# Attention's causal mask: added in place to the kept row F instead of by matmuls, with masks, minima and exponentials issued at high priority

## The chip, the core and the metric

The kernel runs on one core of one Trainium2 chip. The core has a matrix engine, TensorE (PE, with its weight loads shown apart as PEld), a vector engine, VectorE (DVE), a scalar engine, ScalarE (ACT), a general engine, GpSimd (POOL), a synchronisation engine, SyncE (SP), from whose queue most transfers are issued, and 16 DMA engines. Work lies in SBUF (128 partitions) and in PSUM, where PE writes its products. The metric is the device time of one execution in microseconds (us). A profile is one further execution, recorded by the hardware profiler.

## What is computed

One layer with two branches over a sequence of 1024 positions and a width of 1024: a Mamba-2 state-space branch and an attention branch with a forget gate, merged by sigmoid gates, projected and normalised. The change is in the attention branch only, which has 16 heads of 64:

```python
def _forgetting_attention(q, k, v, log_f):
    ...
    fcum = jnp.cumsum(log_f, axis=-1)
    ...
        s = jnp.einsum('bhqd,bhkd->bhqk', q[:, :, q0:q1], k[:, :, :q1]).astype(jnp.float32) * scale
        s = s + fcum[:, :, q0:q1, None] - fcum[:, :, None, :q1]
        qpos = q0 + jnp.arange(ATT_BLOCK)
        kpos = jnp.arange(q1)
        s = jnp.where(kpos[None, :] <= qpos[:, None], s, -jnp.inf)
        prob = jax.nn.softmax(s, axis=-1)
        outs.append(jnp.einsum('bhqk,bhkd->bhqd', prob.astype(v.dtype), v[:, :, :q1]))
```

F is `fcum`, the running sum of the log forget gate. The term F[t] of the query is the same for a whole row of the softmax and drops out of it; what is left is the row -F[s] over the keys, and the mask: a key later than the query counts for nothing. With blocks of 128 queries only the block on the diagonal needs the mask, and there it is always the same triangle.

## The kernel before, and the names that the change touches

**Order of the work.** Tile, the framework, schedules instructions per engine by priority and by estimated times; priority is the order in the program unless `tc.high_priority()` raises it. Some instructions are kept in program order on their engine: `mm` (matmuls, all recorded at line 130), `turn` (transposes on PE, line 133) and whatever stands in `pin(...)`. So PE's order is written out by hand, while ACT, DVE and POOL are arranged by the scheduler around it.

**The weight stream.** All projections go through `Stream`, a list of steps with seven products each (a Strassen scheme in 2 x 2 blocks). `half()` issues half a step: six matmuls of 128 x 512. Their weights are made just before: the weight or a sum of weights (`raw`, `sum`; lines 357, 373 and 381) is split into a high part `wop` (line 351, ACT) and a low part (line 352, DVE). The inputs are split alike (`x6h` and its kin; lines 280 and 281). Results in PSUM (`pb`, `pc`, `pd`) are taken out by `keep` (line 404, ACT, tile `s` in SBUF) and `give` (lines 412 on ACT, 414 to 418 on DVE).

**The attention loop.** Attention and the stream share PE. The loop runs over 48 groups: 8 head pairs `hp` (heads 2 hp and 2 hp + 1, in the two halves of the partitions, e = 0, 1) with six groups g each. A group has two query blocks i (u = 0, 1) and one half h of the keys (512 of them):

```python
GROUPS = [((7, 6), 1), ((7, 6), 0), ((5, 4), 1), ((5, 4), 0), ((3, 2), 0), ((1, 0), 0)]
```

The groups g = 0, 2, 4 and 5 of every pair hold the diagonal: 32 groups, 64 blocks i, 128 tiles of scores. Their widths are 512 (u = 0) and 384 (u = 1) for g = 0 and 4, and 256 and 128 for g = 2 and 5; the other groups have two widths of 512. For each group, in this order:

- `scores` (line 1438) for u = 0, then for u = 1. For both heads: three matmuls (high by high, high by low, low by high) into a PSUM tile `s` (four buffers, shared with the transposes' `pt`). On the diagonal two more in bfloat16 per head: `far` by `eye`, which add 1e30 (scores are kept with their sign turned) to the keys beyond the query, the last 128 columns of the width. Then line 1466 on DVE: it adds the row of F, `fb`, writes the sum to `ex` and its minimum over the row to `nm`. Then line 1470 on ACT: the exponential of `nm - ex`, in place, with its sum to `sm`.
- `fill(m, 0)`: two or three halves of the stream on PE, while DVE and ACT do the minima and the exponentials.
- `turned` (line 1472): transposes of `ex` on PE into `pt`, copied to `p` by ACT (line 1501) or DVE (line 1499). A transpose for u needs that block's exponential.
- `fill(m, 1)`: further halves, and in the next turn of the loop `weighted`, the product of `p` with the values.

**F.** `load_k` loads keys and, last, `fb[hp, h]`: the two heads' rows of F, 512 wide, the same for all partitions (128 x 2 x 512, 512 KB), by line 1335 on SP's queue. There is one buffer for each h. `load_k(hp + 1, 1)` is called at g = 2 and `load_k(hp + 1, 0)` at g = 5, in `loads`, which is called before `turned`. `load_q` (line 1326) loads queries; tiles x4l and the like are inputs of the stream, loaded at line 265.

**Setting up the mask.** Before the loop `eye` (an identity moved by 64 rows, so that each head's half of the partitions can contract it) and `far` (a triangle of 1e30) are made by two memsets, two `affine_select` on POOL and four copies.

Of the kernel before, what the change touches and what calls it, by code (L numbers as in the profile page):

```python
# [8 lines left out]
F32 = mybir.dt.float32  # L9
F32R = mybir.dt.float32r  # L10
BF16 = mybir.dt.bfloat16
AF = mybir.ActivationFunctionType
ALU = mybir.AluOpType
# [3 lines left out]
P = 128  # L17
# [9 lines left out]
NEG = -1.0e30  # L27
# [59 lines left out]
def hybrid_layer(ctx: ExitStack, tc, a, out):  # L87

    nc = tc.nc
# [5 lines left out]
    ident = const.tile([P, P], F32, name="ident")  # L95
# [33 lines left out]
    def mm(*args, **kw):  # L129
        return tc.keep_in_program_order(nc.tensor.matmul(*args, **kw))  # L130
# [4 lines left out]
    def pin(op):  # L135
        return tc.keep_in_program_order(op)

    def small(name="th"):
        return gp.tile([P, HALF], F32, tag="th", name=name)
# [316 lines left out]
    class Stream:  # L456
# [73 lines left out]
        def half(self):  # L530
            if self.run is None:
                if self.at == len(self.steps):
                    return False
                p, which = self.steps[self.at]
                if which == 7 and p.ops is ops_a and "merged" not in fin:
                    return False
                if p.ops is ops_a and not all(p.ops.ready(OPERAND[which].strip("-"), j) for j in range(KH)):
                    return False
                self.ahead(False)
                for ops in self.building:  # L540
                    ops.some(OPERAND[which])
                self.run = p.do(which)
                next(self.run)
            else:
                for _ in self.run:
                    pass
                self.run = None
                p, which = self.steps[self.at]
                if p in self.following:
                    ops = self.following[p]  # L550
                    if ops not in self.building:
                        self.building.append(ops)
                    ops.open(OPERAND[which])
# [581 lines left out]
    with tc.tile_pool(name="pro", bufs=1, reuse_waits="tile", side="right") as pro, tc.tile_pool(  # L1135
        name="prop", bufs=1, space=PSUM, reuse_waits="tile", side="right"
# [114 lines left out]
    with tc.tile_pool(name="ssm", bufs=1, reuse_waits="tile", side="right") as sp, tc.tile_pool(  # L1251
        name="ssmp", bufs=1, space=PSUM, reuse_waits="tile", side="right"
# [42 lines left out]
    with tc.tile_pool(name="att", bufs=1, reuse_waits="tile", side="right") as ap, tc.tile_pool(  # L1295
        name="attp", bufs=1, space=PSUM, reuse_waits="tile", side="right"
    ) as pp:
        rows = [slice(64 * e, 64 * e + 64) for e in range(2)]

        eye = ap.tile([P, 192], BF16, name="eye")  # L1300
        far = ap.tile([P, 192], BF16, name="far")
        nc.vector.memset(eye, 0.0)
        big, beyond = small("big"), small("beyond")
        nc.vector.memset(big[:, 0:192], -NEG)
        for e in range(2):
            nc.vector.tensor_copy(eye[rows[e], 64:P], ident[rows[e], rows[e]])
            nc.gpsimd.affine_select(
                beyond[:, 192 * e : 192 * e + 192], big[:, 0:192], [[1, 192]], ALU.is_gt, 0.0, base=64 * e - 64,
                channel_multiplier=-1,
            )  # L1310
            nc.vector.tensor_copy(far[rows[e], :], beyond[rows[e], 192 * e : 192 * e + 192])

        corner = [(eye[:, 64:192], far[:, 64:192]), (eye[:, 0:P], far[:, 0:P])]

# [5 lines left out]
        q, k, v, fb = {}, {}, {}, {}  # L1320

        def load_q(hp, pair):

            t = ap.tile([P, 2, 256], F32R, tag="q", bufs=2, name="q")
            for n, dram in enumerate((qh_dram, ql_dram)):
                nc.sync.dma_start(t[:, n, :].bitcast(F32), dram[hp, :, pair[1] * P : pair[1] * P + 256])
            q[hp, pair] = t

        def load_k(hp, h):

            t = k[hp, h] = ap.tile([P, 2, HALF], F32R, tag=f"k{h}", name="k")
            for n, dram in enumerate((kh_dram, kl_dram)):
                nc.sync.dma_start(t[:, n, :].bitcast(F32), dram[hp, :, half(h)])
            f = fb[hp, h] = ap.tile([P, 2, HALF], F32, tag=f"fb{h}", name="fb")
            nc.sync.dma_start(f, f_dram[2 * hp : 2 * hp + 2, half(h)].unsqueeze(0).to_broadcast([P, 2, HALF]))

        def load_v(hp, h):
            v[hp, h] = ap.tile([P, 4, P], F32, tag=f"v{h}", name="v")
            pin(nc.sync.dma_start(v[hp, h], v_dram[hp][:, 4 * h : 4 * h + 4, :]))
# [98 lines left out]
        def scores(hp, g, u):  # L1438

            pair, h = GROUPS[g]  # L1440
            i = pair[u]
            w = min(HALF, (i + 1) * P - h * HALF)
            s = [pp.tile([P, HALF], F32, tag="s", bufs=4, name="s") for e in range(2)]
            t, keys = q[hp, pair], k[hp, h]
            isl = slice(i % 2 * P, i % 2 * P + P)
            ops = [(t[:, x, isl], keys[:, y, 0:w]) for x, y in ((0, 0), (0, 1), (1, 0))]
            diagonal = h == i // 4
            for m, (x, y) in enumerate(ops):
                for e in range(2):
                    mm(  # L1450
                        s[e][:, 0:w], x[rows[e]], y[rows[e]], start=(m == 0), stop=(m == 2 and not diagonal),
                        skip_group_check=True,
                    )
            if diagonal:
                for n, (x, y) in enumerate(corner):
                    for e in range(2):
                        mm(
                            s[e][:, w - P : w], x[rows[e]], y[rows[e]], start=False, stop=(n == 1),
                            skip_group_check=True,
                        )  # L1460
            hd = heads[hp]
            for e in range(2):
                o = ex[:, e, u, 0:w]
                nm = hd.at(hd.nm, i, h, e)
                pin(
                    nc.vector.tensor_tensor_reduce(  # L1466
                        o, s[e][:, 0:w], fb[hp, h][:, e, 0:w], 1.0, 3.0e38, ALU.add, ALU.min, nm
                    )
                )
                pin(nc.scalar.activation(o, o, AF.Exp, scale=-1.0, bias=nm, accum_out=hd.at(hd.sm, i, h, e)))  # L1470

        def turned(hp, g, sent):

# [46 lines left out]
        def fetched(name, j):  # L1520
            y = small("y")
            nc.sync.dma_start(y, ops_a.block(name, j))
            return y

        def difference_tile():
            return ap.tile([P, HALF], F32, tag="x", bufs=1, name="x")
# [44 lines left out]
        def loads(m):  # L1571

            hp, g = divmod(m, 6)
            more = hp + 1 < NK
            if g == 0:
                if hp:
                    load_v(hp, 0)
                if not m:

                    for j in range(KH):  # L1580
                        stream.line += ops_s.differences(j, difference_tile, small)
            if g == 1:
                load_q(hp, (3, 2))
            if g == 2 and more:
                load_k(hp + 1, 1)
            if g == 3:
                load_q(hp, (1, 0))
                if more:
                    load_v(hp + 1, 1)
                if hp >= KH:  # L1590
                    state["t"] = difference_tile()
                    nc.sync.dma_start(state["t"], ops_a.block("t1", hp - KH))
            if g == 4 and more:
                load_q(hp + 1, (7, 6))
            if g == (5 if more else 4) and hp >= KH:
                state["y"] = fetched("b11", hp - KH)
            if g == 5 and more:
                load_k(hp + 1, 0)
                load_q(hp + 1, (5, 4))
# [12 lines left out]
            load_v(0, h)  # L1612
        for _ in range(14):
            stream.half()

        weights = (1.1, 1.1, 1.1, 1.1, 0.75, 0.95, 1.05, 0.85)

# [10 lines left out]
        for m in range(6 * NK + 1):  # L1628
# [9 lines left out]
            hp, g = divmod(m, 6)  # L1638
            if not g:
                heads[hp] = Heads(hp)  # L1640
            for u in range(2):
                scores(hp, g, u)
# [86 lines left out]
```

## Time and profile before

| | before |
|---|---|
| median of 3 runs | 1298.21 us |
| lowest and highest run | 1296.74, 1300.02 us |
| the profiled execution, device time | 1301.24 us |
| its span in the trace | 1299.5 us |
| mean granted clock of TensorE in it | 0.995 |
| stage with the attention loop | about 686 to 1140 us |
| mask matmuls (first 687.0, last 1136.7 us) | 256, 18.4 us busy |
| minima, line 1466 | 192, 95.7 us busy on DVE |
| exponentials, line 1470 | 192, 116.0 us busy on ACT |

In the rows below, a group of instructions is given by line, engine, operation, out<-in by the program's names and the shape; "x256" is the number of instructions. Rows of a timeline begin with the start in us from the span's start and the duration (of x instructions run together, overlaps not counted twice); a bracket at their end gives the idle time just before on that engine and the instruction that ended it. "216/221/229" are shortest, median and longest duration in ns. Rows of the chain of waits give start, length and what the end of the kernel was waiting for in that time.

### The profile page before, as it was taken

Reading aid. Unit: us, or ns where it says so; the run is one execution under the profiler, and the core shown is the slowest. Engines: PE = TensorE matmul, PEld = TensorE weight load, DVE = VectorE, ACT = ScalarE, POOL = GpSimd, SP = SyncE. Lnnn points to the kernel's source line nnn. Section 1 sums busy time; section 2 is a strip of 40 time slices with the busy share of each in tenths; the row PEclk is TensorE's granted clock in tenths of the full one; section 3 lists DMA queues with packets and bytes.
Section 4 is the critical chain, followed back from the end, with each engine's and each line's share of the span. In section 5 each row is a group of like instructions: output and inputs, shape, how many; then the busy total and the mean of one; then the engine's idle time right before and its main releaser. Section 6 shows DMA issues by size and latency. Waiting matters only on the chain.

```text
span 1299.5 us, 20991 instructions
## 1 busy us (share of the span) xinstructions
PE 1257.2 (97%) x7054; PEld 984.8 (76%) x7054; DVE 1002.6 (77%) x1994; ACT 789.0 (61%) x1738; POOL 260.1 (20%) x250
## 2 busy tenths in 40 slices
PE   5999999999999999999999999999999999899997
PEld 3678878887888888878877777777667777678786
DVE  7989886897788888897676666766687677786875
ACT  7745665565665666576546566566675566653654
POOL 3000430014300331024001121110001102146052
PEclk9999999999999999999999999999999999999999
DMA  8233553645345633563275675676776668556932
GB/s 295 74 109 76 160 149 95 189 157 173 129 134 187 186 122 113 195 187 125 101 261 171 191 229 180 205 244 198 264 228 224 218 189 295 187 181 196 360 113 98
DMA packets 153515, 233.57 MB, mean 180 GB/s; under 512 B 15968, under 2 KB 61504, under 8 KB 153408
## 3 DMA queue, kind: packets, MB, share of 16 engines
q1 hardware_dynamic: 137408, 197.14, 47.8%
q10 hardware_dynamic: 11136, 19.11, 3.9%
q0 software_dynamic: 4864, 15.99, 3.1%
q8 instruction: 55, 0.90, 0.3%
q14 instruction: 52, 0.43, 0.1%
HBM read 162.99 MB, written 72.34 MB: 181 GB/s over the span
## 4 chain that ended last, share of the span: by engine, by line
PE 72%; DVE 11%; ACT 7%; DMA 6%; issue 3%; SPq 1%; ACTq 0%; DVEq 0%; POOL 0%; POOLq 0%
PE pb L130 31%; PE pc L130 17%; PE pd L130 5%; PE av L130 5%; PE pt L133 4%; PE s L130 4%; ACT ex L1470 2%; PE yps L130 2%; DVE wop L352 2%; DVE sum L357 1%; ACT wop L351 1%; DMA xt<-in_x 1%; DMA raw<-in_wu 1%; DVE ex L1466 1%; DVE xs L771 1%
## 5 line engine op out<-in xcount | busy, mean ns | idle before, releaser
L1470 ACT ACTIVATE ex<-ex,nm 128x512 f32<-128x512 f32 (+1 forms) x192 | 116.0, 606 | 129.9 <-DVE nm L1466 129.8
L352 DVE TENSOR_TENSOR wop<-sum,wop 128x512 fp32r<-128x512 f32 x180 | 137.2, 764 | 59.5 <-ACT wop L351 57.8
L351 ACT ACTIVATE wop<-sum 128x512 fp32r<-128x512 f32 x180 | 112.3, 625 | 100.2 <-DVE sum L357 49.6
L404 ACT ACTIVATE s<-pb 128x512 f32<-128x512 f32 x144 | 85.0, 591 | 87.9 <-PE pb L130 84.3
L352 DVE TENSOR_TENSOR wop<-raw,wop 128x512 fp32r<-128x512 f32 x144 | 103.6, 720 | 43.1 <-ACT wop L351 41.9
L130 PE MATMUL pc<-x3h,wop 128*128 128x512 f32 x384 | 131.9, 401 | 1.4 <-DVE th L414 1.0
L130 PE MATMUL pb<-x0h,wop 128*128 128x512 f32 x384 | 131.8, 400 | 0.0
L130 PE MATMUL pb<-x5h,wop 128*128 128x512 f32 x384 | 129.4, 396 | 1.5 <-ACT s L404 1.5
L130 PE MATMUL pb<-x6h,wop 128*128 128x512 f32 x384 | 129.2, 395 | 1.3 <-ACT s L404 1.3
L130 PE MATMUL pc<-x2h,wop 128*128 128x512 f32 x384 | 130.1, 397 | 0.0
L130 PE MATMUL pb<-x4h,wop 128*128 128x512 f32 x384 | 129.4, 395 | 0.0
L1466 DVE CUSTOM_DVE_ANT_0 ex<-s,fb 128x512 f32<-128x512 f32 (+1 forms) x192 | 95.7, 552 | 36.1 <-PE s L130 36.1
L351 ACT ACTIVATE wop<-raw 128x512 fp32r<-128x512 f32 x144 | 89.6, 623 | 13.4 <-PE pd L130 6.4
L130 PE MATMUL pd<-x1h,wop 128*128 128x512 f32 x288 | 96.3, 394 | 0.0
L130 PEld LDWEIGHTS pc<-x3h,wop 128*128 128x128 f32 x384 | 73.2, 191 | 19.3 <-DVE th L414 1.5
L130 PEld LDWEIGHTS pb<-x5h,wop 128*128 128x128 f32 x384 | 72.1, 188 | 19.2 <-ACT s L404 2.6
L130 PEld LDWEIGHTS pc<-x2h,wop 128*128 128x128 f32 x384 | 72.1, 188 | 17.8 <-issue 2.5
L130 PEld LDWEIGHTS pb<-x6h,wop 128*128 128x128 f32 x384 | 72.2, 188 | 17.6 <-ACT s L404 1.7
L130 PEld LDWEIGHTS pb<-x0h,wop 128*128 128x128 f32 x384 | 72.7, 189 | 16.7 <-issue 1.6
L133 PE MATMUL pt<-ident,ex 128*128 128x128 f32 x576 | 76.7, 277 | 8.2 <-ACT ex L1470 7.8
L130 PEld LDWEIGHTS pb<-x4h,wop 128*128 128x128 f32 x384 | 72.1, 188 | 16.5 <-issue 1.4
L133 PEld LDWEIGHTS pt<-ident,ex 128*128 128x128 f32 x576 | 65.6, 141 | 19.9 <-ACT ex L1470 14.0
(310 smaller groups left out, 2910.5 us busy)
## 6 DMA issues: line engine op xcount, KB each, us to landing
raw<-in_wu SPq DMA_DIRECT2D x128, 256.0 KB
csb<-cs_dram SPq DMA_DIRECT2D x32, 256.0 KB
fb<-f_dram SPq DMA_DIRECT2D x16, 512.0 KB
rb<-st_dram SPq DMA_DIRECT2D x48, 128.0 KB
wd<-in_wo SPq DMA_DIRECT2D x40, 128.0 KB
xt<-in_x SPq DMA_DIRECT2D x8, 512.0 KB
gs_dram<-th ACTq DMA_DIRECT2D x16, 256.0 KB
qh_dram<-th ACTq DMA_DIRECT2D x16, 256.0 KB
```

The source lines that it names most:

```text
L130: return tc.keep_in_program_order(nc.tensor.matmul(*args, **kw))
L133: return tc.keep_in_program_order(nc.tensor.transpose(out_, in_, idn))
L351: nc.scalar.activation(op[:, 0], src, AF.Copy)
L352: nc.vector.tensor_tensor(op[:, 1], src, op[:, 0], ALU.subtract)
L357: self.adds.tensor_tensor(t, x, y, ALU.add)
L404: nc.scalar.activation(s, ps, AF.Copy)
L771: nc.vector.scalar_tensor_tensor(d, u[:, o + j : o + j + HALF], cw[:, tile_idx, j : j + 1], d, ALU.mult, ALU.add)
L1466: nc.vector.tensor_tensor_reduce(o, s[e][:, 0:w], fb[hp, h][:, e, 0:w], 1.0, 3.0e38, ALU.add, ALU.min, nm)
L1470: pin(nc.scalar.activation(o, o, AF.Exp, scale=-1.0, bias=nm, accum_out=hd.at(hd.sm, i, h, e)))
```

## The change

The mask matmuls and their constants go. Instead one triangle `beyond` (128 x 128, 0 up to the diagonal, 1e30 after it) is added in place to the 128 columns of `fb` that belong to the block's diagonal, for both heads in one instruction (128 x 2 x 128). F is the same for all query blocks, but the mask isn't: block i = 7 and block i = 6 read the same tile `fb`, and what is masked for 6 (columns 256 to 383) must still be open for 7. So the blocks with u = 0 (7, 5, 3, 1) have their corner masked ahead of the group, on GpSimd, from `loads`; those with u = 1 (6, 4, 2, 0) on VectorE between the minima of u = 0 and their own. Each is 32 adds. They and the minima and exponentials of all groups (not only the diagonal ones) keep program order on their engine; the VectorE adds, the minima and the exponentials are issued at high priority.

```diff
-        eye = ap.tile([P, 192], BF16, name="eye")
-        far = ap.tile([P, 192], BF16, name="far")
-        nc.vector.memset(eye, 0.0)
-        big, beyond = small("big"), small("beyond")
-        nc.vector.memset(big[:, 0:192], -NEG)
-        for e in range(2):
-            nc.vector.tensor_copy(eye[rows[e], 64:P], ident[rows[e], rows[e]])
...
-        corner = [(eye[:, 64:192], far[:, 64:192]), (eye[:, 0:P], far[:, 0:P])]
+        beyond = ap.tile([P, P], F32, name="beyond")
+        big = small("big")
+        nc.vector.memset(big[:, 0:P], -NEG)
+        nc.gpsimd.affine_select(beyond, big[:, 0:P], [[1, P]], ALU.is_gt, 0.0, base=0, channel_multiplier=-1)
...
+        def corner(hp, i, engine):
+
+            f = fb[hp, i // 4][:, :, i % 4 * P : i % 4 * P + P]
+            pin(engine.tensor_tensor(f, f, beyond.unsqueeze(1).to_broadcast([P, 2, P]), ALU.add))
...
-            diagonal = h == i // 4
             for m, (x, y) in enumerate(ops):
                 for e in range(2):
                     mm(
-                        s[e][:, 0:w], x[rows[e]], y[rows[e]], start=(m == 0), stop=(m == 2 and not diagonal),
-                        skip_group_check=True,
+                        s[e][:, 0:w], x[rows[e]], y[rows[e]], start=(m == 0), stop=(m == 2), skip_group_check=True,
                     )
-            if diagonal:
-                for n, (x, y) in enumerate(corner):
-                    for e in range(2):
-                        mm(
-                            s[e][:, w - P : w], x[rows[e]], y[rows[e]], start=False, stop=(n == 1),
-                            skip_group_check=True,
-                        )
             hd = heads[hp]
+            if u and h == i // 4:
+                with tc.high_priority():
+                    corner(hp, i, nc.vector)
             for e in range(2):
                 o = ex[:, e, u, 0:w]
                 nm = hd.at(hd.nm, i, h, e)
-                pin(
-                    nc.vector.tensor_tensor_reduce(
-                        o, s[e][:, 0:w], fb[hp, h][:, e, 0:w], 1.0, 3.0e38, ALU.add, ALU.min, nm
+                with tc.high_priority():
+                    pin(
+                        nc.vector.tensor_tensor_reduce(
+                            o, s[e][:, 0:w], fb[hp, h][:, e, 0:w], 1.0, 3.0e38, ALU.add, ALU.min, nm
+                        )
                     )
-                )
-                pin(nc.scalar.activation(o, o, AF.Exp, scale=-1.0, bias=nm, accum_out=hd.at(hd.sm, i, h, e)))
+                    pin(nc.scalar.activation(o, o, AF.Exp, scale=-1.0, bias=nm, accum_out=hd.at(hd.sm, i, h, e)))
...
             hp, g = divmod(m, 6)
             more = hp + 1 < NK
+            if g in (1, 3, 4):
+                corner(hp, {1: 5, 3: 3, 4: 1}[g], nc.gpsimd)
+            if g == 4 and more:
+                corner(hp + 1, 7, nc.gpsimd)
...
         for _ in range(14):
             stream.half()
+        corner(0, 7, nc.gpsimd)
```

More of the change, by code (lines that the diff above doesn't have):

```diff
@@ L1298, in hybrid_layer @@
         rows = [slice(64 * e, 64 * e + 64) for e in range(2)]
-        eye = ap.tile([P, 192], BF16, name="eye")
-        far = ap.tile([P, 192], BF16, name="far")
-        nc.vector.memset(eye, 0.0)
-        big, beyond = small("big"), small("beyond")
-        nc.vector.memset(big[:, 0:192], -NEG)
-        for e in range(2):
-            nc.vector.tensor_copy(eye[rows[e], 64:P], ident[rows[e], rows[e]])
-            nc.gpsimd.affine_select(
-                beyond[:, 192 * e : 192 * e + 192], big[:, 0:192], [[1, 192]], ALU.is_gt, 0.0, base=64 * e - 64,
-                channel_multiplier=-1,
-            )
-            nc.vector.tensor_copy(far[rows[e], :], beyond[rows[e], 192 * e : 192 * e + 192])
-        corner = [(eye[:, 64:192], far[:, 64:192]), (eye[:, 0:P], far[:, 0:P])]
+        beyond = ap.tile([P, P], F32, name="beyond")
+        big = small("big")
+        nc.vector.memset(big[:, 0:P], -NEG)
+        nc.gpsimd.affine_select(beyond, big[:, 0:P], [[1, P]], ALU.is_gt, 0.0, base=0, channel_multiplier=-1)
         GROUPS = [((7, 6), 1), ((7, 6), 0), ((5, 4), 1), ((5, 4), 0), ((3, 2), 0), ((1, 0), 0)]
@@ L1464, in scores @@
                 nm = hd.at(hd.nm, i, h, e)
-                pin(
-                    nc.vector.tensor_tensor_reduce(
-                        o, s[e][:, 0:w], fb[hp, h][:, e, 0:w], 1.0, 3.0e38, ALU.add, ALU.min, nm
-                    )
-                )
-                pin(nc.scalar.activation(o, o, AF.Exp, scale=-1.0, bias=nm, accum_out=hd.at(hd.sm, i, h, e)))
+                with tc.high_priority():
[3 more added lines that the diff above has]
+                        )
+                    )
+                    pin(nc.scalar.activation(o, o, AF.Exp, scale=-1.0, bias=nm, accum_out=hd.at(hd.sm, i, h, e)))
         def turned(hp, g, sent):
```

## The prediction

> **What bounds the kernel now.** The page first: totals, granted clock, chain of waits.
>
> ```profile
> span 1299.5 us, 20991 instructions
> PE 1257.2 (97%) x7054; PEld 984.8 (76%) x7054; DVE 1002.6 (77%) x1994; ACT 789.0 (61%) x1738; POOL 260.1 (20%) x250
> ...
> PEclk9999999999999999999999999999999999999999
> ...
> PE 72%; DVE 11%; ACT 7%; DMA 6%; issue 3%; SPq 1%; ACTq 0%; DVEq 0%; POOL 0%; POOLq 0%
> ```
>
> TensorE (PE) is busy 97% of the span at full clock; the rest of the chain is short waits of PE for VectorE (DVE), ScalarE (ACT) and DMA. Next the table by windows, for the attention stage (686 to 1140 us), where the change acts. Its columns: length, busy time of PE, weight loads, DVE, ACT and GpSimd (POOL), granted clock, DMA share, GB/s.
>
> ```profile
> 686.00:910.00 224.00, 223.25 (x1528) 170.07 (x1527) 148.45 (x400) 139.52 (x352) 34.75 (x41) 1.00 0.62 201
> 910.00:985.00 75.00, 68.49 (x452) 48.62 (x450) 60.19 (x157) 53.43 (x135) 4.33 (x8) 0.98 0.74 248
> 985.00:1083.00 98.00, 97.20 (x683) 73.26 (x685) 67.02 (x194) 58.82 (x157) 8.69 (x17) 1.00 0.64 209
> 1083.00:1140.00 57.00, 51.43 (x350) 36.44 (x346) 41.86 (x109) 38.24 (x100) 11.48 (x14) 0.97 0.68 227
> 921.00:924.60 3.60, 1.47 (x6) 0.67 (x6) 1.89 (x8) 2.55 (x8) 0.00 (x0) 1.00 1.04 391
> 925.62:929.04 3.42, 3.42 (x12) 2.38 (x12) 2.67 (x4) 1.52 (x5) 0.00 (x0) 0.50 0.92 335
> ```
>
> Two stretches are bound by PE without gaps (first and third row: 0.75 and 0.80 us idle): time taken off PE there is time won, and any wait put into PE is time lost. In the other two PE idles 6.5 and 5.6 us; there the chain ACT, DVE and DMA decides. The last two rows: after 3.6 us in which PE idles 2.1, the granted clock is 0.50 for 3.42 us, which costs 1.7 us. That happens twice in the attention now.
>
> **What is removed: the mask on PE.** The chain of waits and PE's timeline, for heads 0 and 1 (s: scores; far, eye: mask; pb: the weight stream that follows):
>
> ```profile
> 686.22 1.73 PE s L130 x20
> ...
> 696.99 1.59 PE s L130 x12
> ...
> 707.89 1.15 PE s L130 x20
> ```
>
> ```profile
> L130 PE MATMUL s<-far,eye 64*128 64x128 bf16 x256 | 18.4, 222 | 0.0
> ```
>
> ```profile
> 686.15 0.97 PE L130 MATMUL s<-k,q 64*128 64x512 f32 x6
> 686.96 0.29 PE L130 MATMUL s<-far,eye 64*128 64x128 bf16 x4
> 687.05 0.77 PE L130 MATMUL s<-k,q 64*128 64x384 f32 x6
> 687.66 0.29 PE L130 MATMUL s<-far,eye 64*128 64x128 bf16 x4
> 687.87 0.50 PE L130 MATMUL pb<-x4h,wop 128*128 128x512 f32 x1
> ```
>
> 256 mask matmuls stand in 32 groups, 8 in each; busy 18.4 us, but a record lasts longer than the room it takes. From the start of a mask to the next stream's start is 0.09 us (686.96 to 687.05) and 0.21 us (687.66 to 687.87): 0.30 us per group. Below: 1.73 us (widths 512 and 384 with masks) less 1.59 us (512 and 512 without) is 0.14, too little since 384 is shorter than 512. Above: scaling 1.59 by width gives 1.39 and 0.60 us for the two kinds, so 0.34 and, for the narrow kind (256 and 128, 1.15 us), 0.55, too much since a short matmul has fixed parts. I take 0.30, the value read directly. The two stretches without gaps hold 16 and 7 groups: 23 x 0.30 = 6.9 us won (3.2 to 10). The other nine have a third of that at most, 0.9 us, because PE waits there anyway.
>
> **What is added: 32 adds on DVE, 32 on GpSimd.** No such add runs before; the nearest rows:
>
> ```profile
> L694 DVE TENSOR_TENSOR t<-t x7: 414/418/426, 70.6 to 78.8; 128x256 f32<-128x256 f32 x7
> L850 DVE TENSOR_TENSOR m<-m,cbm x32: 675/770/1789, 138.0 to 616.9; 128x512 f32<-128x512 f32 x32
> ```
>
> ```profile
> L893 POOL TENSOR_TENSOR new<-new,cdec 128x256 f32<-128x256 f32 x24 | 21.9, 914 | 0.0
> ```
>
> ```profile
> 1118.69 1.66 POOL L373 TENSOR_TENSOR sum<-sum,raw 128x512 f32<-128x512 f32 x1 [7.03 <-DVE wop L352]
> ```
>
> ```profile
> 1126.17 0.72 ACT L1470 ACTIVATE ex<-ex,nm 128x512 f32<-128x512 f32 x1 [3.82 <-DVE nm L1466]
> ```
>
> The DVE add has the same 256 elements a partition: 0.42 us. It stands between the second and the third minimum, while ACT is in the first two exponentials of 0.71 us, so it delays the third by some 0.1 us at widths 512 and 384: hidden where the transposes have slack, and counted below where they have none. Without that cover all 32 would cost 13 us. The GpSimd add is 0.91 us. In the built order every one of them stands at least 5 us ahead of its use, but two; the nearer of these (heads 14 and 15, block 3) stands behind the sum of 1118.69, so it ends near 1121.3, 4.9 us ahead of the exponential at 1126.17 that it feeds through a minimum. That cover is worth some 4 us: nothing is added. L850 shows another price: a DVE add with two SBUF operands lasts 675 ns alone and up to 1789 ns in the stage where GpSimd works. Such DVE work beside a GpSimd add (L352 above all) can be held by up to that add's 0.9 us. Where PE is bound this hides; in the other two stretches some nine adds could cost 0 to 8 us. I take 0 for the sum, since few of the DVE's instructions there fall beside one, and keep it as a rival.
>
> The Trainium skill's page "SBUF — State Buffer", section "Who interferes with whom", states it as a rule against this change: a DVE instruction with two SBUF inputs and a GpSimd instruction that reads SBUF shut each other out for a whole instruction. By that rule each of the 32 GpSimd adds could stop the DVE once; the L850 row agrees with it.
>
> **What is moved: the last exponentials.** This decides. "High priority" does not merely bring work forward. In the built order the first two exponentials and the minima stand where they did, with few exceptions, but in 13 of the 16 groups of widths 512 and 384 the last two exponentials, which now depend on the DVE add, stand behind other ACT work: the stream's evictions (s or th from pb) and the first halves of the next weights (wop). The transposes of the second block wait for exactly those two. Heads 0 and 1, key half 1, ACT and then PE:
>
> ```profile
> 690.46 0.71 ACT L1470 ACTIVATE ex<-ex,nm 128x512 f32<-128x512 f32 x1
> ...
> 691.76 0.60 ACT L1470 ACTIVATE ex<-ex,nm 128x384 f32<-128x384 f32 x1
> ...
> 692.36 0.58 ACT L404 ACTIVATE s<-pb 128x512 f32<-128x512 f32 x1
> 692.84 0.62 ACT L351 ACTIVATE wop<-raw 128x512 fp32r<-128x512 f32 x1
> ```
>
> ```profile
> 692.09 1.84 PE L133 MATMUL pt<-ident,ex 128*128 128x128 f32 x14
> ```
>
> The s eviction takes 0.48 us from start to start (692.36 to 692.84) and wop 0.52 (692.84 to the next at 693.36). Put ahead of the third exponential, they make the last end near 693.4 instead of 692.37. The transposes start at 692.09, 0.3 us earlier without masks, and the fourth of the 14 needs the last exponential, so they now wait about 1.2 us. The same sum for the other groups of the stretches without gaps: 0.5 (heads 2, 3), 0.5 and 0.6 (one group each of heads 12, 13 and 14, 15), 0.1 and 0.2 at key half 0 of heads 2, 3 and 6, 7, nothing where the exponentials end 1.5 us or more ahead of the transposes. Together 3.1 us (0, if ACT gets to them while it would be idle, to 5).
>
> In the two stretches where PE waits, the insertions are longer:
>
> ```profile
> 963.84 1.14 ACT L280 ACTIVATE x6h<-x6l 128x512 fp32r<-128x512 f32 x2
> 964.88 0.58 ACT L404 ACTIVATE s<-pb 128x512 f32<-128x512 f32 x1
> ```
>
> ```profile
> 964.03 1.69 PE L133 MATMUL pt<-ident,ex 128*128 128x128 f32 x14
> ```
>
> ```profile
> 1128.19 0.57 ACT L412 ACTIVATE th<-pb 128x512 f32<-128x512 f32 x1
> 1128.67 0.62 ACT L351 ACTIVATE wop<-raw 128x512 fp32r<-128x512 f32 x1
> ```
>
> ```profile
> 1129.94 1.76 PE L133 MATMUL pt<-ident,ex 128*128 128x128 f32 x9 [1.27 <-ACT ex L1470]
> ```
>
> The last fences show the price already: heads 14 and 15 have th and wop ahead of the last exponential today, and PE waits 1.27 us for it. For heads 8 and 9, key half 0, the built order puts s, wop and the two x6h casts (1.04 us from 963.84 to 964.88) ahead of the last exponential: 0.48 + 0.52 + 1.04 = 2.04 us, less some 0.5 of slack, is 1.55. With 1.4 and 0.8 for two more groups of heads 8 and 9, 0.7 for heads 10 and 11, and 0.5 for heads 14 and 15: 5.0 us (2 to 7). Against that stand 0.9 us of masks, 0.6 of minima issued earlier in one group of heads 8 and 9, and a load:
>
> ```profile
> 911.37 0.38 SPq L1335 DMA_DIRECT2D fb<-f_dram  x1
> 911.85 1.89 SPq L265 DMA_DIRECT2D x4l<-t_s  x4
> ```
>
> On SP's queue the 512-KB load of F moves behind these four; at 335 to 391 GB/s (windows) it takes 1.3 to 1.6 us, so they can land that much earlier; I take 1.0. Net 5.0 - 0.9 - 0.6 - 1.0 = 2.5 us lost. In eight more places that load moves behind q loads or a few others, with some 15 us until its use: nothing.
>
> **Sum.** -6.9 + 3.1 + 2.5 = -1.3 us. The profiled execution took 1301.2 us, so 1299.9; the median of the runs shown, 1298.2, lies 3.0 lower, so 1297.
>
> **Rivals.**
> (A) The displaced exponentials cost little: ACT, busy 61%, gets to them before PE does, and PE's gain stays. For it: ACT has idle time in every group. Against it: the 1.27 us. With stalls of 1.7 us instead of 8.1: -6.9 - 0.9 - 0.6 - 1.0 + 1.7 = -7.7, so 1290.5. Faster.
> (B) The stalls of heads 8 to 11 and 14, 15 pull the granted clock down. Place: the groups at 920 to 980 and 1126. Price: 1.7 us each. Point: about 2.1 us of idle PE within 3.6 us. Stalls of 1.4 to 1.55 us lie just under it. Three more such drops and the upper end of the stalls there (7 for 5, +2) make -1.3 + 5.1 + 2 = +5.8: 1304. Slower. The skill's page "TensorE: Matmul & The Clock Gate", section "Why this matters for your kernels", asks only for no idle gap over about 3 us; by that rule none comes. Here the measurement decides: the quoted drop followed gaps of which none reached 3 us.
> (C) GpSimd's adds hold DVE and so ACT's weights in the two slack-free chains: nine adds by half of 0.91 us, +4: 1301, on the border of what can be told.
> (D) The change does not do what it says, in that the minima hardly move ahead; this is already in the sum.
>
> **How the numbers follow.** 0.3% (3.9 us: below 1294.3, above 1302.1) is about what a measurement of this kernel can tell from no change. Forecast 0.38, its own range 1294 to 1302; A 0.32; B 0.19; C 0.11. Faster: 0.29 of A and 0.03 of the forecast, 0.32. Slower: 0.18 of B, 0.04 of C, 0.05 of the forecast, 0.27. Same: the other 0.41. Range 1290 to 1304, from A less half a microsecond to B.
>
> **What would show it.** Right: score streams of about 1.4 us (512, 384) and 0.85 us (256, 128); transposes of heads 0 and 1 at key half 1 interrupted by about 1 us with ACT's exponential named; PE idle between 686 and 910 up by some 2 us; DVE adds near 0.42 us, GpSimd adds near 0.9. Wrong: no new idle time ahead of transposes (then A), more slices at clock 0.50 (then B), L352 stretched beside the GpSimd adds (then C).

## The result and the profile after

| | before | after |
|---|---|---|
| median | 1297.82 us (4 runs) | 1310.13 us (4 runs) |
| lowest and highest | 1296.74, 1300.02 | 1307.84, 1313.04 |
| profiled execution, its span | 1301.24, 1299.5 | 1313.04, 1311.3 |
| mean granted clock in it | 0.995 | 0.989 |

The ratio is 1.009, with an interval of 1.0067 to 1.0112: the change is slower by 12 us. Measured again later (run e12) it was 1.0083 (1.0053 to 1.0113).

The page after, the same rows as before: totals, granted clock, chain.

```profile
span 1311.3 us, 20615 instructions
...
PE 1258.5 (96%) x6798; PEld 984.9 (75%) x6798; DVE 1031.0 (79%) x2021; ACT 791.7 (60%) x1738; POOL 284.4 (22%) x281
...
PEclk9999999999999999999999999999899999899999
...
PE 65%; DVE 12%; DMA 10%; ACT 7%; issue 4%; SPq 1%; ACTq 0%; POOL 0%; DVEq 0%; POOLq 0%
```

PE's share of the chain falls from 72 to 65%. What takes its place is DMA (6 to 10%), DVE and issue. The windows of the attention stage after, with the same columns as in the prediction:

```profile
686.00:910.00 224.00, 221.42 (x1407) 167.79 (x1405) 164.34 (x415) 139.68 (x352) 47.86 (x57) 1.00 0.63 201
910.00:985.00 75.00, 64.85 (x376) 46.08 (x375) 57.75 (x148) 49.72 (x123) 5.61 (x9) 0.91 0.71 236
985.00:1083.00 98.00, 94.66 (x616) 70.84 (x614) 73.15 (x197) 60.10 (x158) 15.56 (x26) 1.00 0.62 201
1083.00:1140.00 57.00, 50.00 (x303) 35.53 (x297) 45.27 (x111) 35.03 (x91) 12.79 (x16) 0.97 0.72 242
```

PE's idle time in them was 0.75, 6.5, 0.8 and 5.6 us; now it is 2.6, 10.2, 3.3 and 7.0 us. The next rows are PE's timeline of the group that the prediction took as its example:

```profile
686.80 1.50 PE L130 MATMUL s<-k,q 64*128 64x512 f32 x12
688.23 0.50 PE L130 MATMUL pb<-x4h,wop 128*128 128x512 f32 x1
...
692.45 0.38 PE L133 MATMUL pt<-ident,ex 128*128 128x128 f32 x2
693.21 0.33 PE L133 MATMUL pt<-ident,ex 128*128 128x128 f32 x1 [0.38 <-ACT ex L1460]
693.81 1.42 PE L133 MATMUL pt<-ident,ex 128*128 128x128 f32 x11 [0.27 <-ACT ex L1460]
```

The scores take 1.43 us to the next stream's start (686.80 to 688.23) instead of 1.72 (686.15 to 687.87): the 0.29 us were there to be won. But the transposes, one piece before, now stop twice for an exponential. ScalarE in that group, and the instructions of VectorE ahead of its third minimum:

```profile
690.35 0.71 ACT L1460 ACTIVATE ex<-ex,nm 128x512 f32<-128x512 f32 x1
...
691.28 0.60 ACT L404 ACTIVATE s<-pb 128x512 f32<-128x512 f32 x1
691.77 0.62 ACT L351 ACTIVATE wop<-raw 128x512 fp32r<-128x512 f32 x1
692.45 0.61 ACT L1460 ACTIVATE ex<-ex,nm 128x384 f32<-128x384 f32 x1
...
693.06 0.60 ACT L1460 ACTIVATE ex<-ex,nm 128x384 f32<-128x384 f32 x1
```

```profile
690.67 0.69 DVE L357 TENSOR_TENSOR sum<-raw 128x512 f32<-128x512 f32 x1 [0.47 <-DMA raw<-in_wu]
691.28 0.42 DVE L1330 TENSOR_TENSOR fb<-fb,beyond 128x256 f32<-128x256 f32 x1
691.85 0.56 DVE L1456 CUSTOM_DVE_ANT_0 ex<-s,fb 128x384 f32<-128x384 f32 x1
```

s and wop stand between the second and third exponential, as built. They are not what holds this group, though. wop ends at 692.39, and the third minimum, behind a sum of weights and the add on VectorE, only at 692.41: the third exponential could hardly have started sooner. In run e4 below, where s and wop stand behind the last exponential, the transposes of this group still stop twice:

```profile
690.20 0.33 PE L133 MATMUL pt<-ident,ex 128*128 128x128 f32 x1 [0.27 <-ACT ex L1473]
690.80 1.42 PE L133 MATMUL pt<-ident,ex 128*128 128x128 f32 x11 [0.27 <-ACT ex L1473]
```

The add is busy 0.42 us, but it pushes the third minimum by more: in 27 of the 32 groups the third minimum starts 0.61 us after the end of the second (in four others further work stands between, and in one the add itself lasts 0.92 us), where it used to start 0.06 to 0.08 us before that end in 29. So a dependent add between two minima costs 0.69 us of the chain, not 0.42.

Where the time went, by the starts of the groups' scores, in one execution each, counted from the start of the attention loop (worked out from the traces; before: at 686.15 us; differences to before in us):

| from the start of attention to the start of | before | change | no mask (e1) | ScalarE order (e4) | both orders (e5) | + early GpSimd add (e13) | no DVE adds, selects (e14) |
|---|---|---|---|---|---|---|---|
| heads 8 and 9 | 229.92 | -0.7 | -3.9 | -1.3 | -1.3 | -0.6 | -2.3 |
| heads 8 and 9, fourth group | 262.41 | +4.8 | -3.5 | -1.0 | -3.0 | -2.1 | -2.6 |
| heads 10 and 11 | 290.13 | +5.4 | -3.7 | -0.7 | -0.2 | -0.9 | -2.7 |
| heads 14 and 15 | 397.26 | +5.9 | -6.0 | -1.1 | -0.9 | -0.9 | -4.9 |
| the end | 613.39 | +11.1 | -6.1 | +4.9 | +2.0 | -0.6 | -4.9 |

Against before, the change loses in two stretches: 6.1 us with heads 8 and 9, and 5.2 us with heads 14 and 15 and what follows (3.2 and 4.8 in its second trace, e12). These are the two stretches where PE was waiting before as well. With heads 0 to 7 it loses most of what it could have won: 3.9 us in e1, 0.7 here.

Each column is one execution, and these lie from 1.4 us below (e1) to 3.4 us above (before) the median of their runs. Differences of 2 or 3 us between columns can be those of single executions; the sizes below go by the medians and ratios.

### The profile page after: what moved, and what is told of

Its sections match the earlier page's. It is cut to its first block, busy times and chain, and to the rows that moved or that the text cites. A ratio compares the mean times of both kernels' runs of the same rounds, so it can differ in the third digit from the quotient of the medians.

```text
span 1311.3 us, 20615 instructions
## 1 busy us (share of the span) xinstructions
PE 1258.5 (96%) x6798; PEld 984.9 (75%) x6798; DVE 1031.0 (79%) x2021; ACT 791.7 (60%) x1738; POOL 284.4 (22%) x281
## 4 chain that ended last, share of the span: by engine, by line
PE 65%; DVE 12%; DMA 10%; ACT 7%; issue 4%; SPq 1%; ACTq 0%; POOL 0%; DVEq 0%; POOLq 0%
PE pb L130 27%; PE pc L130 15%; PE pd L130 5%; PE pt L133 5%; PE av L130 5%; PE s L130 3%; ACT ex L1460 2%; DVE wop L352 2%; PE yps L130 2%; DVE ex L1456 1%; DVE sum L357 1%; DMA raw<-in_wu 1%; ACT wop L351 1%; DMA xt<-in_x 1%; DMA xr<-in_x 1%
## 5 line engine op out<-in xcount | busy, mean ns | idle before, releaser
L352 DVE TENSOR_TENSOR wop<-raw,wop 128x512 fp32r<-128x512 f32 x144 | 109.9, 765 | 32.4 <-ACT wop L351 32.2
L1456 DVE CUSTOM_DVE_ANT_0 ex<-s,fb 128x512 f32<-128x512 f32 (+1 forms) x192 | 98.4, 553 | 42.8 <-PE s L130 38.3
L133 PE MATMUL pt<-ident,ex 128*128 128x128 f32 x576 | 83.8, 286 | 20.1 <-ACT ex L1460 19.5
L130 PEld LDWEIGHTS pc<-x3h,wop 128*128 128x128 f32 x384 | 73.7, 192 | 19.9 <-DVE th L414 2.0
```

The source lines that it names most:

```text
L133: return tc.keep_in_program_order(nc.tensor.transpose(out_, in_, idn))
L352: nc.vector.tensor_tensor(op[:, 1], src, op[:, 0], ALU.subtract)
L1456: nc.vector.tensor_tensor_reduce(o, s[e][:, 0:w], fb[hp, h][:, e, 0:w], 1.0, 3.0e38, ALU.add, ALU.min, nm)
```

## The experiments

Theory 1 after the result: the adds on VectorE, and the orders built around them, cost the time. Theory 2: the adds on GpSimd cost it, by holding VectorE or by GpSimd's queue. Theory 3, after the traces: the clock, at 0.50 for 23.9 us of the attention instead of 6.8, doubles the price of each stall. All results (e1, e2, e3 and e14 leave masks out and so compute something else; they price the parts):

| run | median us | ratio to before, interval |
|---|---|---|
| change | 1310.13 | 1.0090 (1.0067 to 1.0112) |
| e1 no mask | 1294.54 | 0.9974 (0.9957 to 0.9991) |
| e2 GpSimd adds only | 1297.84 | 0.9996 (0.9980 to 1.0012) |
| e3 VectorE adds only | 1305.68 | 1.0066 (1.0048 to 1.0084) |
| e4 ScalarE order of before | 1304.02 | 1.0053 (1.0036 to 1.0069) |
| e5 both orders | 1302.15 | 1.0032 (1.0015 to 1.0050) |
| e6 both orders, select | 1297.93 | 0.9995 (0.9980 to 1.0010) |
| e7 half by matmul | 1294.83 | 0.9973 (0.9957 to 0.9990) |
| e8 no priority | 1307.47 | 1.0077 (1.0049 to 1.0105) |
| e9 before, gaps filled | 1297.88 | 0.9996 (0.9982 to 1.0010) |
| e10 change, gaps filled | 1307.73 | 1.0072 (1.0050 to 1.0095) |
| e11 half by matmul, gaps filled | 1295.52 | 0.9989 (0.9976 to 1.0001) |
| e12 change again | 1308.56 | 1.0083 (1.0053 to 1.0113) |
| e13 both orders, add placed as the select | 1296.58 | 0.9996 (0.9986 to 1.0007) |
| e14 GpSimd selects only | 1293.83 | 0.9958 (0.9944 to 0.9972) |

**Which adds (e1 to e3).** Against the changed kernel:

```diff
# e1
-            if u and h == i // 4:
-                with tc.high_priority():
-                    corner(hp, i, nc.vector)
# e1, further
-            if g in (1, 3, 4):
-                corner(hp, {1: 5, 3: 3, 4: 1}[g], nc.gpsimd)
-            if g == 4 and more:
-                corner(hp + 1, 7, nc.gpsimd)
...
-        corner(0, 7, nc.gpsimd)
# e2: the first part alone; e3: the second part alone
```

> The changed kernel without any mask add: neither the 32 on VectorE nor the 32 on GpSimd (the scores of keys beyond the query stay open, so part of the computation is left out). What is left of the change is the removal of the 256 matmuls and the priority. All theories: 0.30 us in each of 32 groups, 9.6 us at most, 6.9 us where PE has no gaps, so 1288 to 1291 us against 1298 before. If it stays above 1295, the gain itself was priced wrongly.

> The changed kernel without the 32 adds on VectorE (blocks 6, 4, 2 and 0 stay unmasked, that part is left out); the 32 on GpSimd stay. Theory 1 (the VectorE adds delay the last exponentials, and the order on ScalarE built around them puts stream work ahead): as without masks, 1288 to 1293 us, and no insertion of s and wop between the second and third exponential. Theory 2 (the GpSimd adds hold VectorE or the GpSimd queue): still 1303 us or more.

> The changed kernel without the 32 adds on GpSimd (blocks 7, 5, 3 and 1 stay unmasked, that part is left out); the 32 on VectorE stay, and the order on ScalarE with them. Theory 1: 1307 to 1312 us, as the change. Theory 2: 1300 us or less.

Without any mask 1294.5: the gain is 3.4 to 3.9 us, half of what all theories gave it. The table by groups shows where: the 16 groups of heads 0 to 7 bring 3.9 us, 0.25 to 0.33 at 13 of them by the trace, and heads 8 and 9 bring nothing. With the GpSimd adds alone the gain is gone (3.3 us more than e1), with the VectorE adds alone 11.1 us are lost. Neither run came out as either theory had it. Both theories are right in part; VectorE's adds weigh more.

**The order on ScalarE (e4) and VectorE (e5).** The scheduler's rule is left alone; an edge without a semaphore keeps chosen instructions behind the group's last exponential or minimum:

```diff
# e4
+    behind = {"s": [88, 91, ...], "wop": [208, 215, ...], "cast": [...], "th": [...], "st": [...], "p": [...]}
+    def delayed(kind, op):
+        n = seen[kind] = seen.get(kind, -1) + 1
+        if n in behind.get(kind, ()):
+            tc.add_manual_dep(op.ins, last_exp[-1].ins.name, ...)
+        return op
...
-                nc.scalar.activation(op[:, 0], src, AF.Copy)
+                delayed("wop", nc.scalar.activation(op[:, 0], src, AF.Copy))
# e5, further
+    behind = {"low": [254], "xl": [10, 11], ...}
```

> The changed kernel, complete, with the 35 instructions of ScalarE that stand between the exponentials of one group held behind the fourth of them, as before the change; the adds on VectorE and GpSimd stay. Theory 1a (the displaced exponentials are the cause, the add's own time is covered): 1290 to 1296 us, transposes uninterrupted in the group at 687 us, granted clock down at two places as before. Theory 1b (the VectorE add itself, some 0.7 us between the second and the third minimum, is the cause): 1304 to 1310 us, with the stalls ahead of the transposes as they are. Theory 2: 1305 us or more.

> The run with ScalarE's order of before, and in addition one place mended on VectorE: in the group of heads 8 and 9 with widths 256 and 128 at key half 1, the low part of wop and two x5l parts that stand between the second and third minimum are held behind the fourth. If the stall there (2.5 us idle in the run before, 0.95 before the change, and two periods of half clock after it) comes from that order on VectorE: 3 us less than the 1304 measured, 1300 to 1302 us, and one place less with the clock at 0.50. If it comes from the add itself: 1304 us as before.

With the exponentials in their old order 1304.0, 6.1 us under the change's first measurement and 4.5 under its second, far from the 1290 to 1296 of theory 1a: the displacement is a cause, and not the only one. The edges also move some of VectorE's instructions, so the run is not purely ScalarE's order. Most of what e4 wins by the traces stands in one group, the first of heads 8 and 9 (5.1 and 3.2 us against the two traces of the change); that group had no time at half clock in e4 and 6.8 and 3.4 us of it in those two, so how much of the gain there is the order itself stays open.

What a single displaced exponential is worth can be read in heads 8 and 9, key half 0, the group that the prediction worked out in full. PE in the change, then in e4, then before:

```profile
971.29 1.20 PE L133 MATMUL pt<-ident,ex 128*128 128x128 f32 x9 [1.57 <-ACT ex L1460]
```

```profile
964.43 1.73 PE L130 MATMUL av<-p,v 128*64 128x256 f32 x16 [1.37 <-ACT p L1504]
```

```profile
967.96 1.74 PE L130 MATMUL av<-p,v 128*64 128x256 f32 x16 [0.84 <-ACT p L1501]
```

The stop of 1.57 us is there in the change and gone in e4. But the group is only 0.22 us shorter for it (10.62 instead of 10.85; before 10.28): without the stop PE waits 1.37 us at the next product, for the copies `p`, and before the change it waited 0.84 there too.

At 943 us the trace of the change shows another one. VectorE in the group of widths 256 and 128:

```profile
945.44 0.42 DVE L1456 CUSTOM_DVE_ANT_0 ex<-s,fb 128x256 f32<-128x256 f32 x1
...
945.86 0.68 DVE L352 TENSOR_TENSOR wop<-raw,wop 128x512 fp32r<-128x512 f32 x1
946.46 1.29 DVE L281 TENSOR_TENSOR x5l<-x5l,x5h 128x512 fp32r<-128x512 f32 x2
947.66 0.42 DVE L1330 TENSOR_TENSOR fb<-fb,beyond 128x256 f32<-128x256 f32 x1
948.00 0.42 DVE L1489 COPY p<-pt 128x256 f32<-128x256 f32 x1
948.33 0.28 DVE L1456 CUSTOM_DVE_ANT_0 ex<-s,fb 128x128 f32<-128x128 f32 x1
```

The low parts of a weight and of two inputs, and a copy, stand with the add between the second and third minimum: 2.5 us. That group lasts 3.2 us longer than before in the change (2.5 in its second trace), in e3 and in e4 (3.1), and 0.6 us shorter than before in e5, which holds wop and x5l back. Of these 3.7 us the median shows 1.9: 2.2 us come back three groups on as a new wait (heads 8 and 9 to heads 10 and 11 in the table).

**GpSimd: the instruction or its place (e6, e13, e14).**

```diff
# e6 (on e5)
-            pin(engine.tensor_tensor(f, f, beyond.unsqueeze(1).to_broadcast([P, 2, P]), ALU.add))
+            if engine is nc.gpsimd:
+                pin(engine.affine_select(f, f, [[0, 2], [-1, P]], ALU.is_ge, -NEG, base=0, channel_multiplier=1))
+                return
+            pin(engine.tensor_tensor(f, f, beyond.unsqueeze(1).to_broadcast([P, 2, P]), ALU.add))
# e13 (on e5): the same add, but on GpSimd without pin
+            op = engine.tensor_tensor(f, f, beyond.unsqueeze(1).to_broadcast([P, 2, P]), ALU.add)
+            if engine is nc.vector:
+                pin(op)
```

> As the run with both orders mended, but the 32 masks on GpSimd are written by a select in place with one SBUF operand instead of an add with two. If the add on GpSimd costs because it holds VectorE's instructions with two SBUF operands for its 0.74 us and more: 1 to 3 us less than with both orders alone, and the short VectorE instruction sm ahead of the minima of the group at 1123 us back from 0.62 to 0.1 us. If GpSimd's queue order is the cost: no difference within 1 us.

> The run with the select, complete, with the add put back in its place: instructions and orders on all engines are those of the run with the select (1297.9 us); only the GpSimd instruction is an add with two SBUF operands again. If the add's hold on VectorE was the cost: 1301 to 1303 us, as with both orders mended and the add (1302.2). If it was its place in the GpSimd queue (up to four instructions later there): 1297 to 1299 us.

> The changed kernel without the 32 adds on VectorE (blocks 6, 4, 2 and 0 stay unmasked, that part is left out), with selects instead of adds on GpSimd. If the selects cost nothing: 1293 to 1296 us, as without any mask (1294.5), and what is left of the loss with mended orders, 3.4 us, belongs to the VectorE adds. If GpSimd costs whatever the instruction: 1297 to 1299 us, as with its adds (1297.8).

The select brought 4.2 us, which looked like the hold on VectorE. It was not: in e13 the add is back, in e6's place, and the time stays (1296.6). In the traces e13 differs from e5 in GpSimd's queue alone; the orders on VectorE, ScalarE and PE are the same. The select is built with a register move ahead of it, so that `pin` tied it to that move and no longer to the store or sum traced before; 18 of the 32 masks moved up by one to four instructions in GpSimd's queue. The change's GpSimd and VectorE near heads 14 and 15, then e13's at the same place:

```profile
1129.89 1.65 POOL L373 TENSOR_TENSOR sum<-sum,raw 128x512 f32<-128x512 f32 x1 [7.10 <-DVE wop L352]
1131.51 1.17 POOL L1330 TENSOR_TENSOR fb<-fb,beyond 128x256 f32<-128x256 f32 x1
```

```profile
1130.92 1.17 DVE L281 TENSOR_TENSOR x5l<-x5l,x5h 128x512 fp32r<-128x512 f32 x1
1132.01 0.69 DVE L1374 TENSOR_TENSOR sm<-sm,dd 128x8 f32<-128x8 f32 x1
```

```profile
1113.25 0.74 POOL L1343 TENSOR_TENSOR fb<-fb,beyond 128x256 f32<-128x256 f32 x1 [2.52 <-DVE nm L1471]
1117.84 1.66 POOL L386 TENSOR_TENSOR sum<-sum,raw 128x512 f32<-128x512 f32 x1 [3.85 <-DVE wop L365]
```

```profile
1119.97 0.15 DVE L1389 TENSOR_TENSOR sm<-sm,dd 128x8 f32<-128x8 f32 x1
```

In the change the add stands in the queue behind a sum for which GpSimd waits 7 us on VectorE, and then runs just beside the VectorE chain that leads to the group's minima: x5l takes 1.17 us instead of 0.69, the tiny sm (128 x 8) takes 0.69 us instead of 0.15, and the add itself 1.17 instead of 0.74. Placed early, it meets nothing there. So the two engines do hold each other in this trace. The Trainium skill's page "SBUF — State Buffer" (section "Who interferes with whom") has this as a rule for VectorE instructions with two SBUF inputs beside a GpSimd instruction that reads SBUF, and this trace agrees (0.69 us for sm). It cost time where the queue had made the add late. By e5 and e13 the place is worth 5.6 us of medians, 4.7 by the ratios. With the selects and without VectorE's adds (e14) the time is that of no mask at all, within 0.7 us: here an early GpSimd mask is free. What is left for the VectorE adds once everything is mended is 2.8 us by medians, 4.9 by the ratios (e13 less e14).

**The priority (e8).**

```diff
-                with tc.high_priority():
-                    pin(
+                pin(
...
-                with tc.high_priority():
-                    corner(hp, i, nc.vector)
+                corner(hp, i, nc.vector)
```

> The change, complete, without the raised priority for adds, minima and exponentials. If the priority displaces the exponentials: 1304 us or less. If it is the estimated time of the VectorE add that does it, and the priority changes next to nothing: 1307 to 1313 us, as the change, with the same insertions between the exponentials.

1307.5, with the same insertions between the exponentials: ScalarE's built order is the same, instruction by instruction. The priority does next to nothing. Why the scheduler puts s and wop there is argued only: it seems to take what it holds to be ready, and with the add in front the third exponential is not.

**The clock (e9 to e12).** Idle matmuls ahead of the transposes, into the tile that the transposes then write (the first of two such insertions):

```diff
+                for _ in range(first_fill):
+                    mm(
+                        tile, q[hp, pair][rows[0], 0, 0:P], k[hp, h][rows[0], 0, :], start=True, stop=True,
+                        skip_group_check=True,
+                    )
+                first_fill = 0
```

> The kernel before, complete, with 16 idle matmuls of 64 x 512 and 8 of 64 x 128 (their results are overwritten by the transposes that follow) in the two groups where PE waits before its clock falls to 0.50: heads 8 and 9, and heads 14 and 15. They fill time in which PE waits anyway. If the clock falls because PE has been idle, both places keep the full clock and 2 x 1.7 us come back: 1294 to 1296 us. If the low clock has another cause and idle time alone counts: 1298 to 1300 us.

> The change, complete, with such idle matmuls in the seven groups of heads 8 to 11, 14 and 15 where PE waits 1.3 us and more; orders and adds are untouched. If the clock doubles the price of these stalls: seven periods of 3.4 us at 0.50 become two or three, 1302 to 1306 us. If the stalls alone make the loss: 1308 to 1313 us, since no wait is shortened.

> The change itself once more, beside the run with the filled gaps on the same chip: 1307 to 1313 us by all theories.

> The mixture with 128 mask matmuls and the GpSimd select, complete, with idle matmuls in three groups. If both findings hold they add up: 1294.8 less 3.4, so 1290 to 1293 us. If not: 1294 to 1297 us.

Three of the four came out otherwise than expected. The fill does keep the clock up: none of the attention at 0.50 in e9 and e11, 6.8 us in e10 against 13.7 in e12. The time does not follow: e9 is as before, e10 within 1 us of e12, e11 no better than e7. So theory 3 is not borne out as an account of the loss. The trace of e10 shows where its won time went. Counted from the start of attention, heads 8 and 9 reach their fourth group 5.2 us sooner than in the change (3.7 sooner than in e12), and there ScalarE stands still:

```profile
947.84 0.62 ACT L621 ACTIVATE th<-th 128x512 f32<-128x512 f32 x1
953.37 0.33 ACTq L622 DMA_DIRECT2D ga_dram<-th  x1
953.74 0.72 ACT L1460 ACTIVATE ex<-ex,nm 128x512 f32<-128x512 f32 x1 [5.28 <-DMA fb<-f_dram]
```

A store issued from ScalarE's queue goes out only at 953.37, and the four exponentials of the group wait 5.28 us behind it. By the releaser it went when the load of F landed; what ties the two is not settled. From 948.0 to 953.4 us the 16 DMA engines are busy all the time (shares of 0.96 to 1.06), so here who arrives early waits for transfers. Something like it may be why e1 wins nothing with heads 8 and 9; that was not tried. What the fill itself costs was not measured apart, so that the clock is free is not shown. The record even speaks for a price: in the 82 executions of the kernel before that were timed beside the experiments, the 22 with a mean granted clock of 0.995 or less have a median of 1300.4 us, the 43 with 0.997 or 0.998 one of 1296.6. Which of the two, clock or time, follows the other these numbers do not say.

**A version that beats both (e7).** The blocks with u = 0 in place on GpSimd by the select, those with u = 1 by the old matmuls:

```diff
-            diagonal = h == i // 4
+            diagonal = u and h == i // 4
...
+            if g in (1, 3, 4):
+                corner(hp, {1: 5, 3: 3, 4: 1}[g], nc.gpsimd)
```

> A mixture, complete: blocks 7, 5, 3 and 1 are masked in place on GpSimd by the select, blocks 6, 4, 2 and 0 by the mask matmuls of before (128 instead of 256), no add on VectorE, no raised priority. Theory 1 (the VectorE adds and the orders built around them are most of the loss): half of PE's gain stays, 0.15 us in 23 groups or 3.5 us, and the orders are those of before, so 1293 to 1297 us. If masking in place costs by itself on GpSimd: 1298 us or more.

1294.8, a ratio of 0.9973 (0.9957 to 0.9990): 3.5 us faster than before by the ratio, as worked out ahead, and 15 us faster than the change. No add enters VectorE's chain, and PE keeps half of its gain.

## Why the prediction was wrong, by its own steps

- **The gain on PE: right in size, wrong in how much of it lasts.** 0.30 us per group was measured at 0.29. The forecast counted 6.9 us in the stretches without gaps and 0.9 elsewhere; with no mask at all the median gives 3.9. In that run's one trace heads 0 to 7 bring 3.9 and heads 10 to 13 another 2.3, but the stretch of heads 8 and 9 absorbs its share. So the stretches without gaps gave about what was counted (6.2 of 6.9 us by the trace); the step that failed is to carry it in full to the end. Why the medians show only half stays open; the traced execution of before lay 3.4 us above its median.
- **The VectorE add, "delays the third by some 0.1 us": the size was wrong.** The 0.42 us of busy time came from the right row, but here the dependent instructions did not run end to start: 0.69 us. With ScalarE's order mended (e4), the third exponential starts 1.78 us after the first in eight of the 16 groups of widths 512 and 384, instead of 1.43 before, and later still in seven others. That is 0.35 us, and 0.25 in the narrow groups. With the orders mended the adds are worth 2.8 to 4.9 us; the sum shows no term of its own for them.
- **The displaced exponentials: there, but added up wrongly.** The 13 groups came as built. In five of them (heads 0 to 3 and 12 to 15) the last exponential ends 3.63 us after the first begins, instead of 2.63: 1.0 us later, just what s and wop were to cost. But 0.36 to 0.43 of it is left in e4 with the add alone, so add and insertion overlap. Of the example's stop of 0.65 us, 0.54 is left in e4 and so comes from VectorE's side. And a stop was counted as time lost: the 1.57 us of heads 8 and 9 (forecast 1.55) made their group 0.2 us longer, since PE otherwise waits at the next product. The price, 8.1 us gross, is 3.9 to 6.1 by e4 (ratios and medians, against both measurements of the change).
- **Heads 8 and 9, the group at 943 us: 3.2 us longer (2.5 in e12).** The prediction priced stalls of 1.4 and 0.8 us for two more groups of these heads, by insertions on ScalarE. It had no term for the longer one on VectorE, low parts and a copy ahead of the last minima.
- **The GpSimd add, "that cover is worth some 4 us: nothing is added": this step failed most.** It asked first whether the add would be in time for its reader. In time it was; but it stood late in a queue, in front of a VectorE chain without slack, 4.7 to 5.6 us in all. The prediction had the hold as rival C, at 4 us and a chance of 0.11, and took nine adds by half their length; "I take 0 for the sum" was the choice that failed. That the rival's 4 us come near is luck: by the trace it is few adds, at the places where they are late.
- **Rival B, the clock:** its place was right and its count about so (17 us at half clock expected, 13.7 and 23.9 in the two traces of the change, 6.8 before), its price is not borne out: keeping the clock up brought no time back in the medians.
- **The moved loads: "nothing".** In the run without masks the first group of heads 14 and 15 starts its minima 3.5 us after its scores, not 1.1 as before; VectorE waits 1.80 us there for the load th<-gs_dram, and the products after it stand ahead of the minima. Whether the changed order of the loads on SP's queue makes it late was not tried.

The rows of the whole profile that add it up, PE's transposes and weight loads after (before: 8.2 us idle with 7.8 for the exponentials, and 19.9 with 14.0):

```profile
L133 PE MATMUL pt<-ident,ex 128*128 128x128 f32 x576 | 83.8, 286 | 20.1 <-ACT ex L1460 19.5
...
L133 PEld LDWEIGHTS pt<-ident,ex 128*128 128x128 f32 x576 | 67.9, 145 | 36.6 <-ACT ex L1460 30.6
...
L1330 POOL TENSOR_TENSOR fb<-fb,beyond 128x256 f32<-128x256 f32 x32 | 24.5, 776 | 90.8 <-DVE nm L1456 71.0 <-issue 12.3 <-DMA fb<-f_dram 7.3
```

PE's transposes wait 11.7 us longer for exponentials than before. The last row is the GpSimd add's own: 71 us of its waiting is for the minima that still read the unmasked row, and whatever stands behind it in the queue waits too.

The steps in ratios, times 1298 us: the change +11; ScalarE's order -4 (with what moved on VectorE); VectorE's order in one group -3; GpSimd's place -5, which is level with before; VectorE's adds -5 (e13 to e14), and only there the gain of the matmuls' removal shows.

## What to carry to other kernels

An instruction moved off the busiest engine was paid for here where it landed in a chain, with the start-up between dependent instructions and with the order that a scheduler builds around its estimated delay: compare the built orders of every engine, not only of the one that the trace shows first. An instruction that is in time for its reader can still be late for its neighbours: ask what it stands behind in its own queue, and what runs beside it when it gets out. A stall is not yet lost time: ask what the engine waits for next. Time won ahead of a stage that waits for transfers can be given back there, as in e10.

## What was not expected of the hardware

An add between two reductions on VectorE, in place on a row that both read, cost 0.69 us at a busy time of 0.42. ScalarE's exponentials stood for 5.28 us behind a store issued from its queue. Eight small matmuls of 0.22 us each, 1.8 us of busy time, took up only 0.30 us of PE's stream.
